# Latent attention on two sets of buffers, inverses on GpSimd's queue, and block 1's value, gate and key products in the wide form

## Chip, cores and metric

The kernel runs on one core of one Trainium2 chip. The metric is the time of one launch in microseconds of device time; a measurement is the median of several runs.

## What is computed

Two blocks one after the other on a sequence of 256 tokens with 2048 features, all in float32. The first has two layers, the second one. Cut to what the change touches:

```
u = rmsnorm(h) @ w_in[i]                       # block 1, each of 2 layers
a_val, a_glu, a_z, q, k, v, b_z = split(u)
a  = a_val * sigmoid(a_glu)
ya = silu(layernorm(conv31(a) + conv_b)) * silu(a_z)
yb = window_attention(q, k, v) * silu(b_z)
h  = h + concat(ya, yb) @ w_out[i];  h = h + e * sigmoid(h @ w_pg[i])
...
proj = rmsnorm(x) @ w_in_2                     # block 2
y_rwkv = rwkv7_mixer(...)                      # 16 heads of 64, a scan over tokens
y_mla  = mla_mixer(...)                        # 8 heads of 128, causal attention
x = x + concat(y_rwkv, y_mla) @ w_out_2
x = x + (silu(conv3(h @ w_gate)) * (h @ w_up)) @ w_down
```

## The kernel before

Features lie on the 128 partitions, the 256 tokens along the free dimension; 2048 features are 16 tiles ("k-tiles"). Every float32 product is made of two reduced-precision parts, high and low, of the weight and of the input: high x high, high x low and low x high.

**A product and its chunks.** A product of 256 outputs over 2048 inputs takes its weights in chunks of four k-tiles: SyncE fetches 512 KB into `wraw` (`chunks`, L289), ScalarE casts the high part `whi` (L285), VectorE subtracts it to get `wlo` (L286); there are four `wraw` buffers and three of each part. `lin` (L308) then issues, for each k-tile and each of two output tiles t, three matmuls of 256 columns into one bank: high x high, high x low, low x high (L327 to L329). `wide` (L332) issues for each k-tile and t one matmul of 512 columns, high weights against both parts of the input side by side (L347), and one of 256, low weights against the high part (L350), within a chunk first all high ones, then all low ones. Its result lies in two banks of PSUM, one per t, as two halves that have to be added. The first bank has the tag "lin", of which there are three; the second shares a tag with other work of its phase ("sc" in block 1, where the transposes of the input and the attention's scores use it as well). `fold` (L353) adds the halves: ScalarE copies one (L356), VectorE adds the other (L357), once per t. `add_wide` (L359) adds both to a tile on VectorE alone (L363).

**Block 1** (`layer1`, L502) makes per layer: eight products with `lin` for the values and gates of the convolution (`gated`, L486, multiplies them by the row scale, L494 and L495, and by the sigmoid), one with `lin` for the keys (L533), the value, query and gate products, the convolution's 31 taps on VectorE (L583, 480 instructions in all), the LayerNorm (mean L589 on TensorE, subtraction L593 on VectorE), then the products of the gates, the output and the embedding, all wide.

**Block 2's mixers** (`mixers`, L763) go through four groups G of heads. For each: projections (`rkv_lin`), `rwkv_prepare`, in which `tri_inverse` (L1036) inverts the groups' triangular 32 x 32 matrices, and `rwkv_chunks` (L1067), which walks over the tokens with many small products (pz, pch, po) and ends with the normalization (pgn, L1150) and the gate (pgt, L1163) and a write of the result to `ydr` in memory by GpSimd. `tri_inverse` writes the matrices to memory (xd), reads them back in another layout (eight reads to L), makes 31 steps on VectorE (L1058, L1059), writes the result (four writes to td, L1061) and reads it (Tc, L1063): 14 transfers, issued from ScalarE. Work of different groups and of the attention is put in order by a scheduler, which simulates a timeline, with a higher priority for the recurrence. Each engine and each queue does its work in the order that comes out.

The attention's eight heads are done in four pairs (`mla_pair`, L1249), all in one set of two buffers `mla_s`; a pair ends with the split of its output `yp` into high and low in `Ym`. Then the output projection adds to h, from `h2`, eight column groups of `Ym` (two chunks each), seven of the recurrence's first six k-tiles `Yr` (1.5 chunks each), and, when group 3's result has come back from `ydr` (`load_y(3)`), its two last k-tiles for these seven with `lin`, and the eighth group wide. The feed-forward follows: 44 wide products, and the last product with 512 columns a matmul. Eight large buffers ("x8") are shared by all of these in turn.

Of the kernel before, what the change touches and what calls it, by code (L numbers as in the profile page):

```python
# [18 lines left out]
SEQ = 256  # L19
# [97 lines left out]
class Kern:  # L117
# [214 lines left out]
    def wide(self, w, row0, kts, c0, S):  # L332
# [5 lines left out]
        for r, ks in self.chunks(w, row0, kts, c0, 2):  # L338
# [3 lines left out]
            for u in range(2):  # L342
                for t in range(2):
                    ts = slice(t * 128, t * 128 + 128)
                    for i, k in enumerate(ks):
                        if u == 0:
                            nc.tensor.matmul(ps[t][:], lhsT=hi[:, i, ts], rhs=S.both(k).rearrange("p u c -> p (u c)"),  # L347
                                             start=(k == kts[0]), stop=False)
                        else:
                            nc.tensor.matmul(ps[t][:, :SEQ], lhsT=lo[:, i, ts], rhs=S.hi(k), start=False, stop=(k == kts[-1]))  # L350
# [127 lines left out]
    def silu_pair(self, ps, r2, tag, bufs=2):  # L478

        nc = self.nc  # L480
        z = self.wk.tile([128, 2, SEQ], F32, tag=tag, bufs=bufs, name=self.nm("z"))
        nc.vector.tensor_tensor(z[:], ps[:], r2, ALU.mult)
        nc.scalar.activation(z[:], z[:], AF.Silu)
        return z

    def gated(self, pv, pg, r2, other):  # L486

        nc = self.nc
        sg = self.w1.tile([128, 2, SEQ], F32, tag="sg", name=self.nm("sg"))
# [4 lines left out]
        nc.vector.tensor_tensor(cur, pv[:], r2, ALU.mult)  # L494
        ins = nc.vector.tensor_tensor(sg[:], pg[:], r2, ALU.mult)  # L495
        if other is not None:
            self.behind(ins, other)
# [4 lines left out]
    def layer1(self, i, S, st):  # L502
# [12 lines left out]
        ps = []  # L515
        for j in range(8):
            ps.append(self.lin(w_in, 0, kall, (j % 2) * 1024 + j // 2 * 256, S))
            first = self.lo0
            if j % 2 == 0 and j > 0:
                apads.append(self.gated(*ps[j - 2 : j], r2, first))  # L520
                if (i, j) == (0, 2):
                    self.vectors(0)
                    self.bias_table()
                if i == 0:
                    self.bias_write(j // 2 - 1, self.gate)
        apads.append(self.gated(*ps[6:8], r2, None))
        if i == 0:
            self.bias_write(3, self.gate)
# [1049 lines left out]
```

## Time and profile before

| | us |
|---|---|
| median of 3 runs | 2218.68 (2218.06 to 2219.01) |
| profiled execution | 2222.46 |
| its span, first to last instruction | 2220.7 |
| TensorE busy | 2182.3 (98%) |
| weight loads busy | 1972.0 (89%) |
| VectorE busy | 1698.3 (76%) |
| ScalarE busy | 1186.7 (53%) |
| GpSimd busy | 106.7 (5%) |

The profiled execution is one of its own and took 3.78 us more than the median. Busy time of TensorE counts its matmuls with modelled ends, so neighbours overlap, and what a matmul costs in a dense run is the step from one start to the next. L347 in a row is line 347 of the code above. PE, DVE, ACT, POOL and SP are TensorE, VectorE, ScalarE, GpSimd and SyncE; "ACTq" and "POOLq" are their queues of DMA issues.

### The profile page before, as it was taken

The numbers are of one execution on the slowest core, as the hardware profiler recorded it, in microseconds if no ns is written. First come the engines' busy times: TensorE is split into PE (matmuls) and PEld (weight loads), VectorE is DVE, ScalarE is ACT, GpSimd is POOL, SyncE is SP. The second block draws the span as 40 slices with busy tenths as digits, with TensorE's granted clock in tenths as the row PEclk, the third lists the DMA queues.
The fourth block names the chain that finished last, engine by engine and source line by source line (L and its number), as shares of the span: only waits on it lengthen the run. The fifth ranks groups of instructions, "written<-read, shape, count | busy, mean of one in ns | idle before, by whom it ended". The sixth has DMA issues, their size and how long they took to land.

```text
span 2220.7 us, 37351 instructions
## 1 busy us (share of the span) xinstructions
PE 2182.3 (98%) x14263; PEld 1972.0 (89%) x14263; DVE 1698.3 (76%) x3140; ACT 1186.7 (53%) x1825; POOL 106.7 (5%) x253
## 2 busy tenths in 40 slices
PE   8999999999999999999999999999999999999998
PEld 8999988889999888899999887888888888888887
DVE  6999999778989988787777885777765576556765
ACT  6456746554456555656665655355443444444443
POOL 3100000000000000002100000010000000000000
PEclk9999999999999999999999998999999999999999
DMA  7875556665565466777665433576656666566654
GB/s 232 245 207 165 175 166 223 191 210 179 183 184 167 153 198 212 218 219 222 192 169 140 122 106 102 167 255 203 190 185 195 193 189 190 190 192 189 189 191 141
DMA packets 374514, 412.83 MB, mean 186 GB/s; under 512 B 40456, under 2 KB 327429, under 8 KB 373952
## 3 DMA queue, kind: packets, MB, share of 16 engines
q1 hardware_dynamic: 336464, 366.06, 53.6%
q0 software_dynamic: 10960, 31.79, 4.5%
q10 hardware_dynamic: 26912, 12.60, 2.6%
q8 instruction: 112, 1.84, 0.3%
q14 instruction: 66, 0.54, 0.1%
HBM read 390.47 MB, written 19.92 MB: 185 GB/s over the span
## 4 chain that ended last, share of the span: by engine, by line
PE 93%; DVE 3%; DMA 2%; ACT 1%; issue 1%; ACTq 0%; SPq 0%; DVEq 0%
PE wide L347 30%; PE wide L350 15%; PE lin L327 7%; PE lin L328 7%; PE lin L329 7%; PE lin L1393 3%; PE lin L1394 3%; PE lin L1392 3%; PE dn L1393 2%; PE dn L1394 2%; PE dn L1392 2%; PE po L701 1%; PE lin L1225 1%; PE lin L1223 1%; PE lin L1224 1%; DVE wlo L286 1%
## 5 line engine op out<-in xcount | busy, mean ns | idle before, releaser
L285 ACT CAST whi<-wraw 128x1024 fp32r<-128x1024 f32 (+1 forms) x708 | 724.8, 1026 | 837.7 <-PE wide L347 329.5
L286 DVE TENSOR_TENSOR wlo<-wraw,whi 128x1024 fp32r<-128x1024 f32 (+1 forms) x708 | 843.8, 1193 | 357.2 <-ACT whi L285 341.3
L347 PE MATMUL wide<-xs,whi 128*128 128x512 f32 x2916 | 745.7, 394 | 3.9 <-ACT whi L285 2.0
L347 PEld LDWEIGHTS wide<-xs,whi 128*128 128x128 f32 x2916 | 521.3, 189 | 95.0 <-ACT whi L285 2.5
L350 PEld LDWEIGHTS wide<-xs,wlo 128*128 128x128 f32 x2916 | 402.7, 190 | 33.0 <-DVE wlo L286 1.9
L350 PE MATMUL wide<-xs,wlo 128*128 128x256 f32 x2916 | 416.4, 283 | 0.4 <-DVE wlo L286 0.2
L329 PE MATMUL lin<-xs,wlo 128*128 128x256 f32 x1420 | 404.9, 285 | 2.2 <-DVE wlo L286 2.2
L327 PE MATMUL lin<-xs,whi 128*128 128x256 f32 x1420 | 405.5, 286 | 0.9 <-ACT whi L285 0.9
L328 PE MATMUL lin<-xs,whi 128*128 128x256 f32 x1420 | 404.7, 285 | 0.0
L329 PEld LDWEIGHTS lin<-xs,wlo 128*128 128x128 f32 x1420 | 273.5, 193 | 3.3 <-DVE wlo L286 2.6
L327 PEld LDWEIGHTS lin<-xs,whi 128*128 128x128 f32 x1420 | 273.4, 193 | 3.1 <-ACT whi L285 1.3
L328 PEld LDWEIGHTS lin<-xs,whi 128*128 128x128 f32 x1420 | 273.5, 193 | 1.1 <-issue 0.7
L583 DVE SCALAR_TENSOR_TENSOR cy<-apad,vc_cw,cy 128x256 f32<-128x256 f32 x480 | 229.7, 481 | 7.5
L1393 PE MATMUL lin<-wlo,xs 128*128 128x512 f32 (+1 forms) x304 | 117.7, 387 | 0.5 <-DVE wlo L286 0.5
L1394 PE MATMUL lin<-whi,xs 128*128 128x512 f32 (+1 forms) x304 | 117.0, 385 | 0.0
L1392 PE MATMUL lin<-whi,xs 128*128 128x512 f32 (+1 forms) x304 | 114.1, 386 | 0.2 <-ACT whi L285 0.2
L1393 PEld LDWEIGHTS lin<-wlo,xs 128*128 128x128 f32 x304 | 57.2, 188 | 11.9 <-DVE wlo L286 1.2
L1392 PEld LDWEIGHTS lin<-whi,xs 128*128 128x128 f32 x304 | 57.2, 188 | 11.6 <-ACT whi L285 0.6
L1392 PE MATMUL dn<-whi,xs 128*128 128x512 f32 (+1 forms) x176 | 67.0, 381 | 0.0
L1393 PE MATMUL dn<-wlo,xs 128*128 128x512 f32 (+1 forms) x176 | 67.0, 381 | 0.0
L1394 PE MATMUL dn<-whi,xs 128*128 128x512 f32 (+1 forms) x176 | 67.0, 381 | 0.0
L1394 PEld LDWEIGHTS lin<-whi,xs 128*128 128x128 f32 x304 | 57.2, 188 | 11.0
(540 smaller groups left out, 2374.4 us busy)
## 6 DMA issues: line engine op xcount, KB each, us to landing
wraw<-in_w_in_dram SPq DMA_DIRECT2D x244, 512.0 KB, 4.1
wraw<-in_w_out_dram SPq DMA_DIRECT2D x89, 512.0 KB, 4.2
wraw<-in_ffn_w_gate_dram SPq DMA_DIRECT2D x88, 512.0 KB, 4.4
wraw<-in_ffn_w_up_dram SPq DMA_DIRECT2D x88, 512.0 KB, 3.7
wraw<-in_ffn_w_down_dram SPq DMA_DIRECT2D x87, 512.0 KB, 3.9
wraw<-in_w_pg_dram SPq DMA_DIRECT2D x64, 512.0 KB, 4.3
bt<-btab POOLq DMA_DIRECT2D x32, 192.0 KB, 3.2
btab<-bF ACTq DMA_DIRECT2D x4, 1024.0 KB, 7.9
```

The source lines that it names most:

```text
L285: nc.scalar.copy(hi[:], src)
L286: self.lo = nc.vector.tensor_tensor(lo[:], src, hi[:].bitcast(F32), ALU.subtract)
L327: nc.tensor.matmul(ps[:, t, :], lhsT=h, rhs=xh_, start=((t, k) == first), stop=False)
L328: nc.tensor.matmul(ps[:, t, :], lhsT=h, rhs=xl_, start=False, stop=False)
L329: nc.tensor.matmul(ps[:, t, :], lhsT=l, rhs=xh_, start=False, stop=((t, k) == last))
L347: nc.tensor.matmul(ps[t][:], lhsT=hi[:, i, ts], rhs=S.both(k).rearrange("p u c -> p (u c)"), start=(k == kts[0]), stop=False)
L350: nc.tensor.matmul(ps[t][:, :SEQ], lhsT=lo[:, i, ts], rhs=S.hi(k), start=False, stop=(k == kts[-1]))
L583: prev, tail = tail, nc.vector.scalar_tensor_tensor(y, ap[:, t, k : k + SEQ], cw[:, k : k + 1], y, ALU.mult, ALU.add)
L701: nc.tensor.matmul(po[:, qb, g, :], lhsT=pT[:, kb, qb * 128 : qb * 128 + 128], rhs=vd[:, kb, j, :], start=(kb == 0), stop=(kb == 1))
L1392: nc.tensor.matmul(ps, lhsT=zh, rhs=hi, start=(k == 0), stop=False)
L1393: nc.tensor.matmul(ps, lhsT=zh, rhs=lo, start=False, stop=False)
L1394: nc.tensor.matmul(ps, lhsT=zl, rhs=hi, start=False, stop=(k == nt - 1))
```

## The change

Three parts. `wide` goes through a chunk of odd number with the low part first; start and stop of the accumulation are set by counting. Values, gates and keys of block 1 are wide products and are folded before the multiplication by the row scale. The attention has two sets of buffers, which pairs use in turn; a pair writes its output to `mdr` in memory over GpSimd's queue, and `Ym`, allocated after the pairs, is loaded from there as `Yr` is from `ydr`. The 14 transfers of an inverse are issued from GpSimd.

```diff
@@ wide
+        done = [0, 0]
+        for c, (r, ks) in enumerate(self.chunks(w, row0, kts, c0, 2)):
...
-            for u in range(2):
+            for u in ((0, 1) if c % 2 == 0 else (1, 0)):
...
+                        done[t] += 1
+                        flags = dict(start=(done[t] == 1), stop=(done[t] == 2 * len(kts)))
...
@@ value, gated (before: gated(pv, pg, r2, other))
+    def value(self, pv, r2):
...
+        cur = ap[:, :, 15 : 15 + SEQ]
+        self.fold(cur, pv)
+        nc.vector.tensor_tensor(cur, cur, r2, ALU.mult)
+        return ap
+    def gated(self, ap, pg, r2):
...
-        nc.vector.tensor_tensor(cur, pv[:], r2, ALU.mult)
-        ins = nc.vector.tensor_tensor(sg[:], pg[:], r2, ALU.mult)
+        self.fold(sg, pg)
+        nc.vector.tensor_tensor(sg[:], sg[:], r2, ALU.mult)
@@ layer1
+            ps = self.wide(w_in, 0, kall, (j % 2) * 1024 + j // 2 * 256, S)
...
+        self.fold(kT, self.wide(w_in, 0, kall, 4096, S))
+        nc.vector.tensor_tensor(kT[:], kT[:], r2, ALU.mult)
@@ mixers
-        self.mla_s = self.slot(F32, "mla"), self.slot(F32, "mla")
-        Ym = self.new_split(2)
+        self.mla_s = [(self.slot(F32, "mla"), self.slot(F32, "mla")) for _ in range(2)]
+        self.mdr = self.dr.tile([128, 8, SEQ], F32, name="mdr")
...
+        Ym = self.new_split(2)
+        h2 = [self.slot(F32, "h2") for _ in range(2)]
         Yr = self.new_split(2)
-        h2 = [self.slot(F32, "h2") for _ in range(2)]
...
+        for G in range(4):
+            load_y(G, Ym, self.mdr)
@@ tri_inverse (each of its 14 transfers)
-        nc.scalar.dma_start(xd[:].rearrange("(c q) j i -> (q j) c i", q=4), Lc[:])
+        nc.gpsimd.dma_start(xd[:].rearrange("(c q) j i -> (q j) c i", q=4), Lc[:])
@@ mla_pair
-        s1, s2 = self.mla_s
+        s1, s2 = self.mla_s[hp % 2]
...
-        self.split_pair(Y, 2 * hp, yp)
+        nc.gpsimd.dma_start(self.mdr[:, 2 * hp : 2 * hp + 2, :], yp)
```

**What it moves on TensorE.** The place is the end of the mixers, from the first product that needs group 3's inverse (pz on Ttr) on. Before: pz comes while the last pair's projections (`lin_2271`) and its attention are still ahead, and behind the last gate product (`pgt_2157`) wide products go on to the first `lin` of the last two k-tiles (`lin_2412`).

```order
L1307 MATMUL msc_2247_15379<-rope_10999,mla_2158_14849 128x256
L1082 MATMUL pz_2125_14659<-Ttr_2084_14416,XOc_2074_14311 32x32 x16
L1163 MATMUL pgt_2124_14652<-hg_10888,ga_2123_14649 128x256 x4
L1223 MATMUL lin_2271_15509<-whi_2265_15473,ck_1936_13276 128x256
...
L347 MATMUL wide_2343_15972<-xs_2161_14852,whi_2349_15998 128x512 x2
L1163 MATMUL pgt_2157_14842<-hg_10888,ga_2156_14839 128x256 x4
L347 MATMUL wide_2343_15972<-xs_2161_14852,whi_2349_15998 128x512 x2
...
L350 MATMUL wide_2400_16275<-xs_2281_15589,wlo_2406_16301 128x256 x2
L327 MATMUL lin_2412_16325<-xs_2281_15589,whi_2414_16328 128x256
```

Now: the last pair's attention (`mo_2293`, `mo_2297`) is done around that pz, and what follows are wide products alone (L353 and L355 are the high and the low part; in `wide_2311` the low part of the second chunk comes first).

```order
L1330 MATMUL mo_2293_15068<-mla_2179_14366,mla_2178_14365 128x128
L1331 MATMUL mo_2293_15068<-mla_2179_14366,mla_2178_14365 128x128
L1332 MATMUL mo_2293_15068<-mla_2179_14366,mla_2178_14365 128x128
L1085 MATMUL pz_2143_14173<-Ttr_2102_13930,XOc_2092_13825 32x32 x16
L1330 MATMUL mo_2297_15093<-mla_2179_14366,mla_2178_14365 128x128
L1331 MATMUL mo_2297_15093<-mla_2179_14366,mla_2178_14365 128x128
L1332 MATMUL mo_2297_15093<-mla_2179_14366,mla_2178_14365 128x128
L353 MATMUL wide_2312_15152<-xs_2298_15099,whi_2315_15157 128x512 x4
L355 MATMUL wide_2312_15152<-xs_2298_15099,wlo_2316_15158 128x256 x4
```

Now, the end: the normalization and the gate product of group 3 (`pgt_2175`) stand behind the last wide product, `wide_2424`, and the next row is `lin_2436`, on the two last k-tiles.

```order
L353 MATMUL wide_2423_15803<-xs_2303_15104,whi_2429_15829 128x512 x2
L353 MATMUL wide_2424_15804<-xs_2303_15104,whi_2429_15829 128x512
L1153 MATMUL pgn_2173_14345<-cblk_72,Y_2145_14215 128x128 x4
L353 MATMUL wide_2424_15804<-xs_2303_15104,whi_2429_15829 128x512
L1166 MATMUL pgt_2175_14356<-hg_10402,ga_2174_14353 128x256 x4
L327 MATMUL lin_2436_15854<-xs_2303_15104,whi_2438_15857 128x256
L327 MATMUL lin_2440_15880<-xs_2303_15104,whi_2442_15883 128x256
L327 MATMUL lin_2445_15908<-xs_2303_15104,whi_2447_15911 128x256
```

What moved: attention ahead of chunk 3, and the wide products that stood behind the last gate product ahead of it.

**What it moves on GpSimd's queue.** The place is the same, from the write of group 1's result on. Before, GpSimd issues the results' writes and reads, the gate's weights and h, and nothing of the inverse.

```order
L1166 DMA ydr_10760<-sq_1927_13236 128x512
L833 DMA sq_2285_15614<-ydr_10760 128x512
L1158 DMA ga_2156_14839<-in_rwkv_g2_2_dram 128x256
L1159 DMA ga_2156_14839<-in_rwkv_g2_2_dram 64x256
L1166 DMA ydr_10760<-sq_2117_14620 128x512
L827 DMA h2_2282_15590<-hdr_260 128x2048
L827 DMA h2_2283_15591<-hdr_260 128x2048
L833 DMA sq_2286_15618<-ydr_10760 128x512
L1166 DMA ydr_10760<-sq_2150_14810 128x512
L833 DMA sq_2407_16316<-ydr_10760 128x512
```

Now, around group 3's inverse (td, Tc), which shares the queue with the attention's outputs (mdr) and h2:

```order
L828 DMA h2_2300_15101<-hdr_260 128x2048
L1334 DMA mdr_14367<-mla_2177_14364 128x512
L828 DMA h2_2301_15102<-hdr_260 128x2048
L834 DMA sq_2304_15123<-mdr_14367 128x512
L1334 DMA mdr_14367<-mla_2179_14366 128x512
L834 DMA sq_2305_15127<-mdr_14367 128x512
L1064 DMA td_2096_13847<-T_2099_13860 256x1x32 x4
L1334 DMA mdr_14367<-mla_2177_14364 128x512
L1161 DMA ga_2174_14353<-in_rwkv_g2_2_dram 128x256
L1162 DMA ga_2174_14353<-in_rwkv_g2_2_dram 64x256
L1169 DMA ydr_10274<-sq_2135_14134 128x512
L1066 DMA Tc_2101_13929<-td_2096_13847 128x8x32
```

What moved: the four writes of td stand behind the reads of the first two pairs' outputs, and Tc behind the third pair's and a result's write.

## Rows read from the trace of the kernel before

**Rows 1.** The page of the profiled execution: busy time and share of each engine; the clock that was granted to TensorE in 40 equal slices (tenths of full speed); the chain of work that ended last, by engine and by line.
```profile
PE 2182.3 (98%) x14263; PEld 1972.0 (89%) x14263; DVE 1698.3 (76%) x3140; ACT 1186.7 (53%) x1825; POOL 106.7 (5%) x253
PEclk9999999999999999999999998999999999999999
...
PE 93%; DVE 3%; DMA 2%; ACT 1%; issue 1%; ACTq 0%; SPq 0%; DVEq 0%
PE wide L347 30%; PE wide L350 15%; PE lin L327 7%; PE lin L328 7%; PE lin L329 7%; PE lin L1393 3%; PE lin L1394 3%; PE lin L1392 3%; PE dn L1393 2%; PE dn L1394 2%; PE dn L1392 2%; PE po L701 1%; PE lin L1225 1%; PE lin L1223 1%; PE lin L1224 1%; DVE wlo L286 1%
```

**Rows 2.** Timeline of TensorE in block 1, a product of `lin`: start, duration (pipelined, so longer than the step), line, operation.
```profile
200.05 0.28 PE L328 MATMUL lin<-xs,whi 128*128 128x256 f32 x1
200.17 0.28 PE L329 MATMUL lin<-xs,wlo 128*128 128x256 f32 x1
```

**Rows 3.** Timeline of TensorE in block 1, a product of `wide`; each row is one run of matmuls (x8 is 2 output tiles by 4 input tiles).
```profile
447.83 1.11 PE L350 MATMUL wide<-xs,wlo 128*128 128x256 f32 x8
448.78 2.00 PE L347 MATMUL wide<-xs,whi 128*128 128x512 f32 x8
450.62 1.12 PE L350 MATMUL wide<-xs,wlo 128*128 128x256 f32 x8
453.42 0.28 PE L350 MATMUL wide<-xs,wlo 128*128 128x256 f32 x1
```

**Rows 4.** Timeline of TensorE in the feed-forward's last product, 512 columns each.
```profile
1943.90 0.39 PE L1393 MATMUL dn<-wlo,xs 128*128 128x512 f32 x1
1944.13 0.39 PE L1394 MATMUL dn<-whi,xs 128*128 128x512 f32 x1
```

**Rows 5.** Windows by stage: length, busy time of each engine with its instructions, mean granted clock of TensorE, share of the DMA engines, GB/s. 1120 to 1418 us are the mixers from group 2's inverse on and the attention, 1418 to 1470 the output projection.
```profile
1120.00:1240.00 120.00, 116.22 (x1041) 109.05 (x1039) 92.10 (x284) 71.12 (x128) 7.02 (x17) 0.99 0.51 136
1240.00:1337.00 97.00, 90.70 (x760) 81.77 (x759) 77.36 (x262) 59.75 (x135) 4.78 (x9) 0.93 0.41 113
1337.00:1418.00 81.00, 76.79 (x485) 64.77 (x486) 52.48 (x117) 38.22 (x80) 3.22 (x6) 0.89 0.40 127
1418.00:1470.00 52.00, 51.18 (x312) 44.68 (x310) 41.80 (x78) 24.86 (x39) 4.90 (x9) 1.00 0.63 205
```

**Rows 6.** The same view for block 1's first layer up to the LayerNorm.
```profile
40.00:330.00 290.00, 289.62 (x2066) 272.47 (x2064) 263.93 (x490) 160.25 (x247) 21.45 (x48) 1.00 0.65 192
```

**Rows 7.** The page's costliest groups of instructions: the 512-column matmul of `wide` over the whole span.
```profile
L347 PE MATMUL wide<-xs,whi 128*128 128x512 f32 x2916 | 745.7, 394 | 3.9 <-ACT whi L285 2.0
```

**Rows 8.** Instructions by line, ScalarE: the copy of `fold` in the gates of block 1 (count, busy us, mean ns of one).
```profile
L356 ACT COPY z<-wide 128x256 f32<-128x256 f32 x16 | 5.1, 374 | 0.0
```

**Rows 9.** The same for VectorE: the add of `fold`, and the multiply that reads a product of `lin`.
```profile
L357 DVE TENSOR_TENSOR z<-z,wide 128x256 f32<-128x256 f32 x16 | 6.2, 413 | 0.0
L494 DVE TENSOR_TENSOR apad<-lin,r 128x512 f32<-128x512 f32 x8 | 5.5, 690 | 2.2 <-PE lin L329 1.3 <-ACT r L251 1.0
```

**Rows 10.** The chain, 320 to 345 us: start, duration, work. VectorE's subtraction of the LayerNorm's mean, behind the sums of the convolution.
```profile
327.75 2.48 DVE cy L593 x4
```

**Rows 11.** Window of the first 20 us, TensorE.
```profile
0.00:20.00 20.00, 13.41 (x75) 1.00 0.94 294
```

**Rows 12.** Timeline of TensorE at the start: two matmuls of `lin` at the slower step of the first 14 us.
```profile
13.29 0.41 PE L327 MATMUL lin<-xs,whi 128*128 128x256 f32 x1
13.51 0.41 PE L328 MATMUL lin<-xs,whi 128*128 128x256 f32 x1
```

**Rows 13.** The output tile of group 3 behind its last gate product pgt: by instruction count, durations (min/median/max, ns) and start times (first and last) between 1418 and 1432 us.
```profile
L1165 DVE TENSOR_TENSOR sq<-sq,pgt x1: 690/690/690, 1420.5 to 1420.5; 128x512 f32<-128x512 f32 x1
L1166 POOL DMA_DIRECT2D ydr<-sq x1: 553/553/553, 1421.7 to 1421.7; - x1
L272 DVE TENSOR_TENSOR xs<-sq,xs x1: 692/692/692, 1429.6 to 1429.6; 128x512 fp32r<-128x512 f32 x1
```

**Rows 14.** Timeline of TensorE: the first `lin` on the output of group 3.
```profile
1452.18 0.28 PE L327 MATMUL lin<-xs,whi 128*128 128x256 f32 x1
```

**Rows 15.** Timeline of GpSimd: the issue of a transfer with 256 runs.
```profile
17.46 0.74 POOL L718 DMA_DIRECT2D pr<-in_p_dram  x1
```

**Rows 16.** The inverse's matrix T in memory: its four writes and its read per group, as issued by ScalarE's queue (durations as above).
```profile
L1061 ACTq DMA_DIRECT2D td<-T x16: 571/628/638, 1130.5 to 1326.9; - x16
L1063 ACTq DMA_DIRECT2D Tc<-td x4: 378/385/392, 1137.0 to 1332.1; - x4
```

**Rows 17.** Windows of ten microseconds, TensorE alone: busy time, granted clock.
```profile
1260.00:1270.00 10.00, 8.26 (x71) 0.85 0.67 161
1370.00:1380.00 10.00, 9.81 (x54) 0.69 0.17 49
```

**Rows 18.** The chain, group 3's inverse: the last write of T, its read, and the second of the products (pz) behind it.
```profile
1326.89 5.17 DMA td<-T
1332.08 2.37 DMA Tc<-td
...
1344.56 1.46 PE pz L1094 x30
```

**Rows 19.** Transfers by kind: queue, count, size, median us from issue to landing.
```profile
ydr<-sq POOLq DMA_DIRECT2D x4, 256.0 KB, 3.2
...
L<-xd ACTq DMA_DIRECT2D x16, 32.0 KB, 3.9
...
Tc<-td ACTq DMA_DIRECT2D x4, 128.0 KB, 2.4
```

More of the change, by code (lines that the diff above doesn't have):

```diff
@@ L341, in wide @@
                 hi, lo = self.wsplit(r[:, :n, :], [128, n, 256])
[L342 removed]
+            if ks[0] == kts[0]:
+                self.lo0 = self.lo
+            for u in ((0, 1) if c % 2 == 0 else (1, 0)):
                 for t in range(2):
@@ L345, in wide @@
                     for i, k in enumerate(ks):
+                        done[t] += 1
+                        flags = dict(start=(done[t] == 1), stop=(done[t] == 2 * len(kts)))
                         if u == 0:
-                            nc.tensor.matmul(ps[t][:], lhsT=hi[:, i, ts], rhs=S.both(k).rearrange("p u c -> p (u c)"),
-                                             start=(k == kts[0]), stop=False)
+                            nc.tensor.matmul(ps[t][:], lhsT=hi[:, i, ts], rhs=S.both(k).rearrange("p u c -> p (u c)"), **flags)
                         else:
-                            nc.tensor.matmul(ps[t][:, :SEQ], lhsT=lo[:, i, ts], rhs=S.hi(k), start=False, stop=(k == kts[-1]))
+                            nc.tensor.matmul(ps[t][:, :SEQ], lhsT=lo[:, i, ts], rhs=S.hi(k), **flags)
         return ps
@@ L493, in gated @@
         cur = ap[:, :, 15 : 15 + SEQ]
-        nc.vector.tensor_tensor(cur, pv[:], r2, ALU.mult)
-        ins = nc.vector.tensor_tensor(sg[:], pg[:], r2, ALU.mult)
-        if other is not None:
-            self.behind(ins, other)
+        self.fold(cur, pv)
+        nc.vector.tensor_tensor(cur, cur, r2, ALU.mult)
+        return ap
+    def gated(self, ap, pg, r2):
+        nc = self.nc
+        sg = self.w1.tile([128, 2, SEQ], F32, tag="sg", name=self.nm("sg"))
+        cur = ap[:, :, 15 : 15 + SEQ]
+        self.fold(sg, pg)
+        nc.vector.tensor_tensor(sg[:], sg[:], r2, ALU.mult)
         self.gate = nc.scalar.activation(sg[:], sg[:], AF.Sigmoid)
@@ L514, in layer1 @@
         apads = []
-        ps = []
         for j in range(8):
[L517 to L528, printed above, removed]
+            ps = self.wide(w_in, 0, kall, (j % 2) * 1024 + j // 2 * 256, S)
+            if j % 2 == 0:
+                apads.append(self.value(ps, r2))
+                continue
+            self.gated(apads[-1], ps, r2)
+            if (i, j) == (0, 1):
+                self.vectors(0)
+                self.bias_table()
+            if i == 0:
+                self.bias_write(j // 2, self.gate)
         V = self.v1[i]
-        pk = self.lin(w_in, 0, kall, 4096, S)
         kT = self.w1.tile([128, 2, SEQ], F32, tag="sg", name=self.nm("kT"))
-        nc.vector.tensor_tensor(kT[:], pk[:], r2, ALU.mult)
+        self.fold(kT, self.wide(w_in, 0, kall, 4096, S))
+        nc.vector.tensor_tensor(kT[:], kT[:], r2, ALU.mult)
         half = lambda ap, h: ap[64 * h : 64 * h + 64]
@@ L830, in mixers, with load_y @@
                                                ALU.mult, ALU.mult)
-        def load_y(G):
+        def load_y(G, dst, src):
             yt = self.sqt()
-            nc.gpsimd.dma_start(yt[:], self.ydr[:, 2 * G : 2 * G + 2, :])
-            self.split_pair(Yr, 2 * G, yt[:])
+            nc.gpsimd.dma_start(yt[:], src[:, 2 * G : 2 * G + 2, :])
+            self.split_pair(dst, 2 * G, yt[:])
+        for G in range(4):
+            load_y(G, Ym, self.mdr)
         for G in range(3):
-            load_y(G)
+            load_y(G, Yr, self.ydr)
         def rows(k0, k1, j, Y, row0=0):
@@ L849, in mixers @@
             rows(0, 6, j, Yr)
-        load_y(3)
+        load_y(3, Yr, self.ydr)
         vf = self.vf
```

21 lines of the change are left out of this document (6 added, 15 removed).

## The prediction

> **What bounds the kernel now.** I read the page's busy shares, its 40 slices and the chain first. TensorE is busy for 98% of the span, at nearly full clock, and the chain that ends last is 93% TensorE, two thirds of it the products of `wide` and `lin` [rows 1]. So time can come from three places only: TensorE work that costs less, stretches where TensorE is idle or clocked down, and new stalls of either kind. Then I read the timeline for the step from one matmul to the next, since a busy engine's true price is its cadence: in `lin` a 256-column matmul follows every 0.120 us [rows 2]; in `wide` a chunk of eight 512-column and eight 256-column matmuls comes every 1.84 + 0.95 us, 2.795 from run to run [rows 3]; a dense run of 512-column matmuls has 0.227 us [rows 4]. Last the windows by stage, for idle time and clock: 1120 to 1418 us, mixers and latent attention, is the one long stretch that loses some [rows 5].
>
> **Products made wide.** Eight value and gate products and one key product per layer become wide: 18 products of 4 chunks, 72 chunks. A chunk of `lin` is 24 matmuls, 24 x 0.120 = 2.88 us; a wide one is 2.795, or 2.785 in the alternating order (next part). The difference, 0.085 to 0.095 us, times 72 is 6.1 to 6.8, with the 0.7 that a whole switch fewer would add at most 7.5; I take **-7.0 us**. This is on the path, since nothing but TensorE's own work sets the pace there (289.6 of 290 us busy from 40 to 330 us [rows 6]).
>
> By a rule of the Trainium skill ("TensorE: Matmul & The Clock Gate", section "Back-to-back issue gap") an isolated matmul of N columns takes N/2.4 + 2.5 ns, so a wide pair would save only one 2.5 ns overhead: an estimate of 576 x 2.5 ns = 1.4 us in place of 7. The rows give 0.120 and 0.227, some 13 ns over N/2.4 in each, so the rows decide.
>
> **The alternating order.** Chunk 2 now begins with the low part, on which chunk 1 ended, so a product switches widths half as often. Two switches a chunk cost what a chunk takes beyond its parts: 2.795 - (8 x 0.227 + 8 x 0.120 = 2.776) = 0.019 us. Half of it, 0.0095, over some 365 chunks (2916 recorded 512-column matmuls, 8 a chunk [rows 7]) is 3.5; some runs are cut by other work anyway, so **-3.0 us**. Bounds: 0 (the 0.019 may come from the chunk's own change of weights) and -7 (all of it). That odd chunks ask for the low weights first costs nothing while VectorE's split runs a chunk ahead; if it falls behind, the wait comes before the high half in place of after it, at most 1.84 us earlier each time.
>
> **The fold.** A wide result is in two banks and has to be added up: two ScalarE copies of 0.372 [rows 8] and two VectorE adds of 0.413 [rows 9], against one VectorE multiply of 0.690 that read the bank and stays as a multiply from SBUF. Issued back to back two adds take about 0.74, so 18 products add 13.3 us to VectorE and about 12 to ScalarE, half per layer. ScalarE has the room. VectorE is busy 263.9 of 290 us before the first LayerNorm [rows 6], so 6.7 us fit into 26, but not all of the 26 is free at the right place: the convolution's last sums end just ahead of the LayerNorm, where TensorE already waits behind four 0.68 us operations [rows 10]. Bounds: 0 and all 6.7 us plus the wait, 9 a layer. I take 1 per layer, near the lower end because the row shows slack there, **+2**.
>
> **Start.** Before, 256-column matmuls of `lin` fill TensorE between the input's transposes; it is busy 13.4 of the first 20 us [rows 11]. A wide product's second bank has the tag "sc", which the transposes use too, so it starts after the last transpose: ahead of that one the order had 49 matmuls of `lin` as filler and has 16 of `wide` now. 49 x 0.17 (between the step of 0.12 and the 0.22 of the first 14 us [rows 12]) = 8.3 us against 8 x 0.227 + 8 x 0.12 = 2.8 gives the upper bound, 5.5; the lower is 0, if the input's arrival sets the end anyway. I take the middle, **+2.5**, as no row tells which.
>
> **The mixers.** Three edits act together: two sets of attention buffers, attention's output through memory instead of straight into Ym, and the inverses' 14 transfers each on GpSimd's queue. What can be won: idle time plus (1 - clock) x length in the three windows [rows 5], that is 3.8 + 1.2, 6.3 + 6.8 and 4.2 + 8.9, **31.2 us** in all. The orders of the change show that pairs 1 and 2 are projected earlier and that all attention is over ahead of group 3's second pz, with chunk 3 then woven into dense wide products. A dense stretch of that kind is 1418 to 1470: 51.2 of 52 us busy, clock 1.00 [rows 5]. So of the last 13.1 about 10 go; of the 13.1 before, I take half; of the first 5, half: -10 - 6.5 - 2.5 = -19.
>
> What comes new: before, some 32 us of wide products (1420.5 to 1452.2 us) follow the last gate product pgt, and under them its result is multiplied, written, read back and split. That takes from 1420.5 to 1430.3, 9.8 us [rows 13], and nobody waits for it: the first `lin` on it runs at 1452.18 [rows 14]. In the new order `lin` on just this data follows pgt at once, and no wide product is left. So that latency is exposed, **+9.5** (it was 9.8, of which the last part needs only the second half of the split; bounds 8 and 12, the upper with a clock that falls in the hole).
>
> GpSimd's queue: a transfer's issue takes GpSimd 0.55 us with 128 runs [rows 13] and 0.74 with 256 [rows 15], so about 0.2 us per 128 short runs; ScalarE took 0.57 to 0.64 for 256 and 0.38 for Tc [rows 16]. An inverse has 1024 runs in xd and in Tc, 512 in each of four and 256 in four more: about 13 us of GpSimd, some 7 more than on ScalarE. Bounds: 0, where group 3 is not what the end waits for, and +7. ScalarE in turn is rid of 56 issues of 0.38 to 0.64, some 28 us; that buys between 0 and 5. I let these two cancel. What the moved instructions now stand behind, in one queue: two 1024 KB h2 loads, the mdr writes and their reads, each of which waits for attention. What used to wait behind them on ScalarE's, casts of weights, waits no longer. Mixers together: -19 + 9.5 = **-9.5**.
>
> **The sum.** -7.0 - 3.0 + 2 + 2.5 - 9.5 = -15.0. The profiled execution took 2222.46 us (span 2220.7), so about 2207.5 by its own measure; it stands 3.8 above the median of the three runs, 2218.68. I forecast **2204 us** for the median.
>
> **Rivals.**
> 1. *More is won in the mixers.* If the pairs fill nearly all holes, 28 of the 31.2 us go, and the exposed latency is partly covered by the other columns' wide chunks: 2218.7 - 5.5 - 28 + 7 = about 2192. For it: the clock there is down to 0.69 to 0.85 in ten-microsecond windows [rows 17], and the dense stretch behind them ran at 1.00. Against it: holes ahead of 1240 us come from the chain of the inverses, not from attention.
> 2. *Counts only.* The mixers give nothing net: holes are moved to other places, or the 9.5 us and the 7 of the queue eat the rest; 2218.7 - 5.5 = 2213. For it: most of the 31.2 us lie where several short chains share TensorE, and the trace doesn't show that more buffers would shorten any of them. Against it: the largest loss, 13.1 us after 1337, is beside attention that will be over by then.
> 3. *Slower: group 3's inverse gets stuck in GpSimd's queue.* The order puts two mdr reads and one mdr write, which wait for pairs 0 and 1, ahead of the four td writes, and Tc behind another mdr write and a ydr write. Before, the way from the last td write to the second pz took from 1326.9 to 1344.6 us [rows 18], and the end had 32 us in reserve. Now the end has none: each microsecond by which td or Tc is late shows whole. If pair 1's and 2's outputs are late by a scores-softmax-values round and the reads land 3.2 us later each, Tc is 25 us late, and the time is 2204 + 25 = about 2229. From 15 us of lateness the gain is gone, from 19 it is slower. Against it: pairs 1 and 2 are projected early in the new order.
>    The Trainium skill ("SBUF — State Buffer", section "SBUF: two separate sides") names a mechanism that would do the same: descriptors of GpSimd's transfers are written by GpSimd, which is shut out while VectorE runs certain copies, and it advises ScalarE's queue instead. The trace so far does not bear it out: with VectorE 76% busy GpSimd's transfers land in 3.2 us, ScalarE's in 2.4 to 3.9 [rows 19].
> 4. *VectorE becomes the bound before LayerNorm.* 9 us a layer in place of 1: 2204 + 16 = 2220.
>
> **How the numbers follow.** A measurement of this kernel tells 0.2%, 4.4 us, from no change, so "same" is 2214.2 to 2223.1. Chances: the forecast with its bounds (2198 to 2211) 0.54, rival 1 0.18, rival 2 0.15, rival 3 0.07, rival 4 0.06. Faster: 0.54 + 0.18 + 0.11 of rival 2 = 0.83; same: 0.04 + 0.06 = 0.10; slower 0.07. The range leaves out rival 3 and the far half of rival 1 and of rival 4: 2185 to 2217.
>
> **What would show it.** Right: `lin`'s rows in block 1 gone, the wide cadence 2.78 us in pairs of chunks; TensorE idle some 9 us between pgt and the next `lin`, the one large hole; clock 1.00 through chunk 3's last 70 us. Wrong: TensorE waiting for Ttr (Tc) or for VectorE ahead of cs; a long wait of GpSimd ahead of td; a first wide product that ends past where `lin` did by more than 5 us.

## The result and the profile after

The change takes **2241.2 us** (median of 4 runs, 2239.0 to 2242.7) where the kernel before took 2218.4 beside it: a ratio of 1.0102, with a 95% interval of 1.0089 to 1.0114. The forecast was 2204 (2185 to 2217), so the sign was wrong (forecast -15, measured +22.8). The profiled execution took 2242.3, its span 2240.5.

The page after, to be read against [rows 1]: TensorE does less (2179.9 us in place of 2182.3, 576 matmuls fewer in the records), and yet the span is longer.

```profile
PE 2179.9 (97%) x13687; PEld 1944.6 (87%) x13687; DVE 1715.5 (77%) x3176; ACT 1207.8 (54%) x1861; POOL 146.4 (7%) x317
```

**What went as forecast.** The wide cadence in block 1 (timeline of TensorE, against [rows 3]): two chunks from 453.83 to 459.39, 2.78 us each.

```profile
453.83 3.82 PE L353 MATMUL wide<-xs,whi 128*128 128x512 f32 x16
457.48 2.08 PE L355 MATMUL wide<-xs,wlo 128*128 128x256 f32 x16
459.39 1.78 PE L353 MATMUL wide<-xs,whi 128*128 128x512 f32 x7
```

The latency behind the last gate product, which 32 us of wide products used to cover [rows 14], is exposed: 8.26 us of idle TensorE, then some 23 `lin` matmuls at 0.21 in place of 0.12 us, 2.2 us more, until 1474.05 (in brackets: the idle time of the engine before a row, and what ended it).

```profile
1458.26 2.58 PE L1166 MATMUL pgt<-hg,ga 128*128 128x256 f32 x8 [0.88 <-ACT sq L1158]
1469.10 1.01 PE L327 MATMUL lin<-xs,whi 128*128 128x256 f32 x3 [8.26 <-ACT xs L271]
1474.05 0.34 PE L327 MATMUL lin<-xs,whi 128*128 128x256 f32 x1
```

**What did not.** TensorE in windows of 40 us (length, busy time with its matmuls, granted clock, DMA share, GB/s), first before, then after. In the windows from 1320 and 1440 TensorE is now idle for 9.5 and 9.1 us, where it was for 2.7 and 3.0, and what came free ahead of 1240 is small.

```profile
1120.00:1160.00 40.00, 38.07 (x333) 0.96 0.65 165
1320.00:1360.00 40.00, 37.29 (x287) 0.87 0.55 165
1440.00:1480.00 40.00, 37.04 (x230) 1.00 0.70 231
```

```profile
1120.00:1160.00 40.00, 40.00 (x375) 1.00 0.69 193
1320.00:1360.00 40.00, 30.52 (x210) 0.91 0.51 168
1440.00:1480.00 40.00, 30.87 (x181) 0.87 0.45 143
```

A ledger of the span, worked out from such windows of 20 us: idle TensorE plus (1 - clock) x length, by part of the program. Where a low clock falls on idle time it counts twice, so the last row, the span less all such loss (what little lies outside these parts too), is only near the work's own price.

```
us                      before   alt  wide  ACT queue  after
start, 0 to 40             6.6   6.6   7.7        7.6    7.5
LayerNorm 1, 320 to 380    2.7   2.9   8.7        8.7    8.7
LayerNorm 2, 800 to 860    1.1   1.3   8.4        8.4    7.6
mixers, 1120 to 1520      34.6  17.1  18.7       37.0   46.9
end, from 2140            11.7  13.7  14.2       14.0   15.1
rest of the span        2163.6 2163.0 2156.7  2155.8  2153.8
```

(alt, wide and ACT queue are e_alt, e_wide and e_after_actq below.) From before to after the rest falls by 9.8, about the 10 us of the two count terms; 12.5 come at the LayerNorms, 3.4 at the end, and 12.3 in the mixers, where 9.5 were to be won. How far the last row can be trusted: 0.6 of the 9.8 falls with the alternating order, 6.3 with the wide products, and 2.9 between e_wide and the change, which have the same products; in the kernels below that have the products of e_wide it lies between 2151.9 and 2159.1.

### The profile page after: what moved, and what is told of

The parts are those of the page before. It is cut to its first block, busy times and chain, and to the rows that moved or that the text cites. A ratio compares the mean times of both kernels' runs of the same rounds, so it can differ in the third digit from the quotient of the medians.

```text
span 2240.5 us, 36345 instructions
## 1 busy us (share of the span) xinstructions
PE 2179.9 (97%) x13687; PEld 1944.6 (87%) x13687; DVE 1715.5 (77%) x3176; ACT 1207.8 (54%) x1861; POOL 146.4 (7%) x317
## 5 line engine op out<-in xcount | busy, mean ns | idle before, releaser
L353 PE MATMUL wide<-xs,whi 128*128 128x512 f32 x3492 | 857.6, 394 | 14.3 <-DVE xs L272 8.1
L353 PEld LDWEIGHTS wide<-xs,whi 128*128 128x128 f32 x3492 | 638.5, 189 | 139.1 <-DVE xs L272 8.6
L355 PEld LDWEIGHTS wide<-xs,wlo 128*128 128x128 f32 x3492 | 454.8, 191 | 27.0 <-DVE wlo L286 5.5
L355 PE MATMUL wide<-xs,wlo 128*128 128x256 f32 x3492 | 466.3, 284 | 4.2 <-DVE wlo L286 3.2
L327 PE MATMUL lin<-xs,whi 128*128 128x256 f32 x844 | 241.6, 287 | 8.9 <-ACT xs L271 8.3
L329 PE MATMUL lin<-xs,wlo 128*128 128x256 f32 x844 | 241.8, 287 | 0.0
L328 PE MATMUL lin<-xs,whi 128*128 128x256 f32 x844 | 241.0, 286 | 0.0
L327 PEld LDWEIGHTS lin<-xs,whi 128*128 128x128 f32 x844 | 162.5, 193 | 10.3 <-ACT xs L271 8.7
L329 PEld LDWEIGHTS lin<-xs,wlo 128*128 128x128 f32 x844 | 162.5, 193 | 1.6 <-issue 1.3
L328 PEld LDWEIGHTS lin<-xs,whi 128*128 128x128 f32 x844 | 162.5, 193 | 0.9 <-issue 0.3
```

What stands on the lines that cost most here:

```text
L327: nc.tensor.matmul(ps[:, t, :], lhsT=h, rhs=xh_, start=((t, k) == first), stop=False)
L328: nc.tensor.matmul(ps[:, t, :], lhsT=h, rhs=xl_, start=False, stop=False)
L329: nc.tensor.matmul(ps[:, t, :], lhsT=l, rhs=xh_, start=False, stop=((t, k) == last))
```

## The experiments

The kernel before was run beside each and took 2218.5 to 2220.0; ratios are to it.

**1. The change in layers.** e_alt is the kernel before with the alternating order alone; e_wide adds the wide values, gates and keys and leaves the mixers; e_after_actq is the whole change but for the inverse's queue; e_after_oneset the whole but for attention's sets and its way through memory.

```diff
@@ e_alt, to before
-            for u in range(2):
+            for u in ((0, 1) if c % 2 == 0 else (1, 0)):
...
@@ e_wide, to e_alt
+        self.fold(cur, pv)
+        self.fold(sg, pg)
+            ps = self.wide(w_in, 0, kall, (j % 2) * 1024 + j // 2 * 256, S)
+        self.fold(kT, self.wide(w_in, 0, kall, 4096, S))
...
@@ e_after_actq, to the change (L1047 to L1066)
-            nc.gpsimd.dma_start(td[:, :, q, :], T[32 * q : 32 * q + 32, :, :])
+            nc.scalar.dma_start(td[:, :, q, :], T[32 * q : 32 * q + 32, :, :])
...
@@ e_after_oneset, to the change
-        nc.gpsimd.dma_start(self.mdr[:, 2 * hp : 2 * hp + 2, :], yp)
+        self.split_pair(Y, 2 * hp, yp)
...
```

> The kernel before with the alternating order alone. Theory counts (the order saves half of the width switches, 0.0125 us a chunk as the trace of the change shows, some 365 chunks): 4 to 4.5 us faster, about 2214, and nothing else moved: VectorE's LayerNorm stalls as before. Rival (the mixers' order is sensitive to any change of the products' times): 125 wide matmuls stand behind the last pgt in place of 182, still enough to hide 10 us, so a loss there would speak for the rival.

Measured: 2208.4, 0.9947 [0.9932, 0.9963].

> Alternating order and the wide value, gate and key products, mixers as before. Theory fold (block 1's two LayerNorm stalls, 5 and 6 us longer in the trace of the change, come with the folds on VectorE and ScalarE): -4.5 - 7 + 1.7 (start) + 11.5 = +2, about 2220 with TensorE idle or clocked down some 9 to 10 us around each LayerNorm. Rival (the stalls are only an accident of the full change's order): 2209, stalls of 3 us as before.

Measured: 2215.9, 0.9979 [0.9967, 0.9990].

> The full change with the inverse's 14 transfers back on ScalarE's queue: wide products and two sets of buffers stay. In its order 186 wide matmuls stand behind the last pgt again, in place of 0. Theory queue (moving the transfers made group 3 late and left nothing behind pgt): the 17 us later first lin goes, 2241 - 20 = about 2220 or less, no 8 us hole ahead of the first lin. Rival sets (two sets put the attention ahead of group 3's inverse and make it late whatever the queue): still 2232 or more.

Measured: 2235.3, 1.0067 [1.0052, 1.0083].

> The full change with one set of attention buffers and Ym split directly, as before; wide products and GpSimd's queue stay. In its order 99 wide matmuls stand behind the last pgt, 17 us, enough for the 9.8 us. Theory queue: the inverses are late by the same 13 to 20 us on VectorE, part of it is covered, about 2230. Rival sets: about 2220, group 3's pz back at 1340 to 1350 us.

Measured: 2222.4, 1.0009 [0.9993, 1.0024].

So the steps are -11.7 for the order of chunk parts, +7.5 for the wide products, +19.4 for sets and memory, +5.9 for the queue on top of them (7.8 by the ratios, since the change itself was timed beside another set of runs of the kernel before). e_alt gained nearly three times what was expected. At the LayerNorms e_wide loses 8.7 and 8.4 us in the ledger, as the theory on the fold had it. Of the other two, both came out as the rival on the sets said. Most of the loss is the sets' and memory's, and the fastest kernel of all is e_alt.

**2. Sets or memory?** e_oneset_mem is e_wide with attention's output through memory and one set; e_sets_yrfirst is e_after_actq with the products of Yr, the recurrence's result, ahead of those of Ym, attention's. In both the allocation moves along: Ym's buffers are taken only behind the pairs, in the second behind Yr and h2.

```diff
@@ e_oneset_mem, to e_wide
-        self.split_pair(Y, 2 * hp, yp)
+        nc.gpsimd.dma_start(self.mdr[:, 2 * hp : 2 * hp + 2, :], yp)
...
@@ e_sets_yrfirst, to e_after_actq (its loads load_y are moved likewise)
-        for j in range(8):
-            rows(0, 8, j, Ym, 1024)
...
+        for j in range(8):
+            rows(0, 8, j, Ym, 1024)
```

> Wide products, inverses on ScalarE's queue, one set of attention buffers as before, but the pair's output goes through memory and Ym is allocated after the pairs, as in the change: of the part on latent attention only the second set is taken away. Theory filler (two sets let all four pairs' projections run early, by 1331 us, so that nothing is left to cover the softmaxes and the last inverse): back to the time of the kernel with wide products alone, 2216, within 5 us. Rival round trip (write, read and split of a pair's output, 8 to 10 us each, keep the first products of the output projection waiting): 2228 to 2236, stalls of TensorE between 1320 and 1400 us of 20 us or more.

Measured: 2233.9, 1.0061 [1.0039, 1.0083].

> Wide products, two sets, inverses on ScalarE's queue; the output projection begins with the recurrence's six k-tiles (Yr, in the memory of ck and a recurrence buffer), and the attention's part (Ym) comes second. The first 29 us of wide products then need no attention. Theory filler: TensorE's stalls between 1320 and 1400 us, 33 us with two sets, fall to under 20, and the time from 2235 to 2222 or less. Rival: if the hole is the in-order wait of VectorE for the attention's softmaxes (T's steps stand behind them), it stays at 2230 or more. Only 79 wide matmuls stand behind the last pgt, 13 us, just enough for its 9.8.

Measured: 2227.9, 1.0039 [1.0024, 1.0054].

The way through memory costs nearly what both did (18 us over e_wide, with one set); the second set on top of it adds 1.4, less than these runs can tell. So my theory that two sets let attention run ahead and leave TensorE without filler isn't needed for the 18 us. It isn't refuted either: e_sets_yrfirst came out between what it said (2222 or less) and what its rival said (2230 or more), and two sets without the way through memory weren't tried. What memory does, in e_oneset_mem's list of waits (engine, waiter, releaser: us, times, longest); in e_wide's the first row has 4.5 us, and the second is absent:

```profile
DVE xs L272 <- ACT xs L271: 11.5, 9, 3.2
ACT xs L271 <- DMA sq<-mdr: 10.2, 3, 4.8
```

ScalarE stands at the cast (L271) until the read of `mdr` lands, and VectorE at the subtraction (L272) until the cast is done; what the program has put behind these two, casts and splits of weights among it, stands with them (TensorE's waits for whi and wlo between 1120 and 1520: 8.7 us, in e_wide 4.7).

**3. How much of it is that standing?** Both are e_oneset_mem with Yr first; e_mem_once also reads all of `mdr` in one transfer after the last pair, so that no split stands in line early.

```diff
@@ e_mem_four, to e_oneset_mem: the edit of e_sets_yrfirst
@@ e_mem_once, to e_mem_four
+        nc.gpsimd.dma_start(ya[:], self.mdr[:])
-            load_y(G, Ym, self.mdr)
+            self.split_pair(Ym, 2 * G, ya[:, 2 * G : 2 * G + 2, :])
...
```

> One set of buffers, attention's output through memory in four reads as in the change, wide products, ScalarE's queue; the output projection begins with Yr's products. Companion of the next kernel. With Ym first the same parts took 2234. Theory waits in line (the four splits stand in ScalarE's and VectorE's queues between softmaxes and casts, and each waits 2 to 5 us there for its read): 2226 to 2234, since the splits still stand there. Rival late products (it is the first wide products that wait for Ym): Yr first gives them 29 us of cover, so 2218 or less.

Measured: 2224.6, 1.0024 [1.0012, 1.0037].

> As its companion, but attention's output is read back in one transfer behind the last pair, so that none of the four splits can stand in the queues ahead of the last pair's softmaxes. Theory waits in line: ScalarE's waits on the read between 1320 and 1380 us go, TensorE's stalls from 1320 to 1400 us (22 with Ym first) fall to 10 to 14 and the time to 2216 to 2222, below its companion by 5 or more. Rival late products: no better than the companion, or worse by the longer read.

Measured: 2219.1, 0.9989 [0.9976, 1.0002].

e_mem_four came out between its two expectations, so both have a part; e_mem_once did what the theory said. Of the 18 us, then, some 9 (7.4 in e_sets_yrfirst) go with Ym's products being first in line, 5.5 with splits that wait in the queues, and 3 stay. Each of these edits also changes the scheduler's order, and experiment 5 will show that this alone can move as much; what speaks for the reading is that the wait goes along with the time: ScalarE stands for `mdr` for 10.2 us in e_oneset_mem, for 6.3 in e_mem_four, and not at all in e_mem_once's list. TensorE's window from 1360 tells the same, e_mem_four above e_mem_once:

```profile
1360.00:1400.00 40.00, 36.89 (x235) 0.87 0.37 114
```

```profile
1360.00:1400.00 40.00, 39.29 (x273) 1.00 0.48 158
```

With two sets it isn't that clean. The mixers' loss in the ledger, 1120 to 1520, split into its two parts:

```
us      before  e_alt  e_wide  oneset_mem  mem_four  mem_once  sets_yrfirst  ACT queue  after
idle      17.2   12.1    13.5        21.6      16.9      12.3          14.4       20.0   29.7
clock     17.4    5.0     5.2        15.6      13.8       7.0          17.2       17.0   17.2
```

In the kernels with the way through memory and a loss over e_wide, the change itself excepted, more than half of that loss is a lower granted clock. And e_sets_yrfirst, whose list has no wait of ScalarE for `mdr` and whose TensorE is idle hardly longer than e_wide's, still takes 12 us more than e_wide. By the ledger nearly all of that is clock: from 1330 to 1380 it is at 0.61 to 0.83, between its two levels (1.00 and 0.50, 2.4 and 1.2 GHz), and in the first 20 us of that TensorE was idle for 6.6:

```profile
1330.00:1340.00 10.00, 7.76 (x38) 0.83 0.32 103
1340.00:1350.00 10.00, 5.67 (x20) 0.68 0.17 38
```

Whether the second set or only the order that comes with it makes that hole isn't shown.

**4. The fold.** e_wide_pool has the values' and gates' multiply by the row scale on GpSimd; e_wide_pool_lin also the first product in `lin` again.

```diff
@@ e_wide_pool, to e_wide
-        nc.vector.tensor_tensor(cur, cur, r2, ALU.mult)
+        nc.gpsimd.tensor_tensor(cur, cur, r2, ALU.mult)
-        nc.vector.tensor_tensor(sg[:], sg[:], r2, ALU.mult)
+        nc.gpsimd.tensor_tensor(sg[:], sg[:], r2, ALU.mult)
@@ e_wide_pool_lin, to e_wide_pool
+            if (i, j) == (0, 0):
+                apads.append(self.value(self.lin(w_in, 0, kall, 0, S), r2))
+                continue
...
```

> Alternating order and wide value, gate and key products, mixers as before, with the multiplications of values and gates by the row scale on GpSimd (16 of 128x512). They take 11 us off VectorE, most of what the folds put on it. Theory fold (VectorE's extra work delays the last convolution sums and with them both LayerNorms): TensorE's stalls around 320 to 360 and 800 to 840 us, 9.4 and 8.4 with the folds, go back to 4.5 and 2.3; about 2206 against 2216. Rival (the order of the products and of their ScalarE copies): stalls stay, 2215.

Measured: 2212.8, 0.9973 [0.9958, 0.9988].

> As the kernel with the row scale on GpSimd, with the very first product (values, layer 0) as lin again, whose matmuls fill TensorE between the transposes of the input. Theory start (the wide form's second bank shares its tag with the transposes): stalls in the first 40 us 7 in place of 10.4, 3 us faster than its companion. Rival: the input's arrival sets the end of this stretch, no difference.

Measured: 2212.7, 0.9967 [0.9953, 0.9980].

With VectorE relieved, the loss at the second layer's LayerNorm falls from 8.4 us in the ledger to 3.4 in both kernels. At the first layer's it is cut by half in e_wide_pool (8.7 to 4.6), but back at 9.8 in e_wide_pool_lin, where the clock fell; there more than the fold decides. The windows, e_wide, e_wide_pool and e_wide_pool_lin:

```profile
320.00:360.00 40.00, 34.66 (x197) 30.25 (x196) 34.74 (x70) 23.51 (x41) 3.45 (x8) 0.91 0.52 170
```

```profile
320.00:360.00 40.00, 35.87 (x216) 31.32 (x215) 35.55 (x70) 27.12 (x46) 3.45 (x8) 1.00 0.60 188
```

```profile
320.00:360.00 40.00, 35.39 (x196) 31.23 (x195) 33.67 (x66) 26.13 (x45) 3.42 (x8) 0.87 0.53 171
```

Of the whole time little is left: 3.2 us by the medians, 1.3 by the ratios, whose intervals overlap, where the theory had 10; in the mixers e_wide_pool loses 24.6 us to e_wide's 18.7. The start's `lin` gains nothing that can be measured (0.1 us).

**5. Why is e_alt so good?** By the steps the cadence pays some 4 us; 11.7 came. The feed-forward shows the cadence alone: between the first `dn` of its first and last groups lie 112 wide chunks, which take 476.05 us in the kernel before (1656.68 to 2132.73) and in e_alt_b, 474.93 in e_alt (1643.23 to 2118.16) and e_alt_ac: 0.010 us a chunk, 3.7 for 365. The alternating order in block 1 and the feed-forward alone (e_alt_ac), and in the mixers' stage alone (e_alt_b):

```diff
@@ e_alt_ac and e_alt_b, to e_alt
-            for u in ((0, 1) if c % 2 == 0 else (1, 0)):
+            for u in ((0, 1) if c % 2 == 0 or self.ph == "b" else (1, 0)):
+            for u in ((0, 1) if c % 2 == 0 or self.ph != "b" else (1, 0)):
```

> Alternating order in block 1 and in the feed-forward only; the wide products of the mixers' stage keep high before low. The alternating kernel was 11.7 us faster, of which the steps explain 4.5. Theory order (the products' shorter times let the planner put group 3's chunk differently, 125 wide matmuls behind the last pgt in place of 182; the stalls there fell by 8): this kernel has that order too, so about 2209, stalls from 1320 to 1400 us 9 in place of 21. Rival form (in the mixers' stage itself the alternation lets odd chunks wait less): about 2214 to 2216.

Measured: 2209.9, 0.9954 [0.9939, 0.9969].

> Alternating order in the mixers' stage only (the output projection's wide products, some 30 chunks, 0.4 us by the steps). Its order around group 3 is that of the kernel before (183 wide matmuls behind the last pgt). Theory order: 2218, no difference. Rival form: about 2210, stalls from 1320 to 1400 us 9.

Measured: 2219.0, 0.9999 [0.9989, 1.0010].

e_alt_ac doesn't touch the code of the mixers' stage, and yet their loss in the ledger falls from 34.6 to 17.3 (e_alt_b: 33.9). The scheduler puts another order together: 125 wide matmuls stand behind the last pgt in place of 182; the others run ahead of it. Both came out as the theory on the order said.

**6. The queue by itself.** e_wide with the inverse's way in (xd, L) or out (td, Tc) on GpSimd's queue.

```diff
@@ e_q_in, to e_wide
-        nc.scalar.dma_start(xd[:].rearrange("(c q) j i -> (q j) c i", q=4), Lc[:])
+        nc.gpsimd.dma_start(xd[:].rearrange("(c q) j i -> (q j) c i", q=4), Lc[:])
...
@@ e_q_out, to e_wide
-            nc.scalar.dma_start(td[:, :, q, :], T[32 * q : 32 * q + 32, :, :])
+            nc.gpsimd.dma_start(td[:, :, q, :], T[32 * q : 32 * q + 32, :, :])
...
```

> Wide products and one set of buffers with a direct split (2216 with the inverse on ScalarE's queue, 2222 with all 14 transfers on GpSimd's); here the nine transfers into the inverse (xd, L) are GpSimd's, the five out of it (td, Tc) ScalarE's. In its order VectorE's first T step stands 21 to 25 rows behind Lc for groups 1 to 3, 10 to 12 with all on ScalarE's queue. Theory order (the planner expects these transfers later than they come, and VectorE does other rows first): most of the 6 us, 2219 to 2223; the first T step of group 2 some 5 us or more later behind Lc than the 14.3 with ScalarE's queue, and without a wait, since L has landed. Rival transfers out (the reads and writes of T are what is late): 2216 to 2217.

Measured: 2236.7, 1.0080 [1.0065, 1.0095].

> The reverse: xd and L on ScalarE's queue, td and Tc on GpSimd's. First T steps 9 to 11 rows behind Lc, as with all on ScalarE's queue. Theory order: 2214 to 2218. Rival transfers out: 2220 or more, with the way from td to Ttr longer by 2 us or more a group.

Measured: 2223.9, 1.0028 [1.0016, 1.0039]; its runs lie between 2217.8 and 2227.6, and the profiled one is the first of these, so that its trace doesn't show the median.

The way in costs 20.7, the way out 8, and both together 6.5 (e_after_oneset against e_wide). A price per transfer would add up; these don't. Neither theory fits both kernels: e_q_in is slower than either said, e_q_out is where the rival had it. In the traces 9 to 13 of VectorE's rows lie between a group's Lc and its first step T with ScalarE's queue (groups 1 to 3), 27 to 37 with all on GpSimd's, 22 to 26 in e_q_in, 9 to 12 in e_q_out: the scheduler places the chain anew each time. In e_q_in's trace TensorE stands for group 3's Ttr, for 6.94 us (in e_wide 0.9 for all four groups): T's four writes, on ScalarE's queue as in e_wide, land 3.4 to 9.4 us after they are issued (e_wide: 2.4 to 3.7), and Tc is read only then:

```profile
1358.81 1.73 PE L1082 MATMUL pz<-Ttr,XOc 32*32 32x32 f32 x32 [6.94 <-DVE Ttr L1064]
1358.31 0.45 DVE L1064 STREAM_TRANSPOSE Ttr<-Tc 128x256 f32<-128x256 f32 x1 [7.71 <-DMA Tc<-td]
```

Why they land that late isn't shown.

## Why the prediction was wrong

**Right.** The counts: 2.78 us a chunk measured, 0.010 us a chunk for the alternating order (forecast 0.0095), and the rest of the span 9.8 shorter (forecast 10). That last match is in part luck, as the ledger tells this row to 3 or 4 us only. From e_alt to e_wide the rest falls by 6.3 (forecast 7.0). By the estimate from the Trainium skill's "TensorE: Matmul & The Clock Gate" ("Back-to-back issue gap") the wide products would save 1.4 us; the rows were the better guide. The start: +0.9 in the ledger (forecast +2.5, bounds 0 and 5.5). The exposed latency: 8.3 idle + 2.2 of clock (forecast 9.5, bounds 8 to 12).

**Mis-sized: the fold.** Forecast +1 a layer; the ledger has +6.0 and +6.5, inside the bound of 9; they come with the wide products (e_alt to e_wide: +5.8 and +7.1). In the trace after, ahead of the first LayerNorm, VectorE has hardly a gap and is late with wlo and with cy; TensorE waits:

```profile
326.42 0.74 PE L355 MATMUL wide<-xs,wlo 128*128 128x256 f32 x4 [1.02 <-DVE wlo L286]
330.23 0.70 PE L589 MATMUL cs<-cy,cblk 128*128 128x256 f32 x2 [0.72 <-DVE cy L583]
333.58 0.38 PE L1226 MATMUL lin<-pp,whi 128*128 128x256 f32 x1 [2.66 <-ACT ev L741]
```

The 26 us of slack were a mean over 290 us; at that place there was none, which the four operations of [rows 10] had already said. (The 0.372 us of a fold's copy is 0.374 in [rows 8]; nothing hangs on it.) The queue, whose two terms were left to cancel, cost 5.9 to 7.8 us on top of the rest.

**The step that failed** is "So of the last 13.1 about 10 go; of the 13.1 before, I take half", the -19 of the mixers. In the ledger the loss there didn't shrink to some 25 (34.6 - 19 + 9.5) but grew to 46.9; without the exposed latency, some 36 in place of 15.6. It was argued from what the two sets free. What wasn't priced is the way through memory, put at nothing in the sum: its split is an instruction in ScalarE's queue and one in VectorE's, placed by a simulated timeline, and when the read lands later than that, all behind it waits. The chip's timeline of VectorE after, group 3's T steps (L1061, L1062) among the scaling of h (L830) and the splits (L272):

```profile
1336.48 0.22 DVE L1061 TENSOR_TENSOR Tt<-L,T 128x66 f32<-128x66 f32 x1
...
1338.34 3.25 DVE L830 SCALAR_TENSOR_TENSOR h<-h,vc_a,rf 128x256 f32<-128x256 f32 x8
...
1341.97 0.22 DVE L1062 TENSOR_TENSOR T<-T,Tt 128x66 f32<-128x66 f32 x1
...
1342.70 0.68 DVE L272 TENSOR_TENSOR xs<-sq,xs 128x512 fp32r<-128x512 f32 x1
...
1345.07 0.21 DVE L1061 TENSOR_TENSOR Tt<-L,T 128x48 f32<-128x48 f32 x1
1348.42 0.69 DVE L272 TENSOR_TENSOR xs<-sq,xs 128x512 fp32r<-128x512 f32 x1 [3.15 <-ACT xs L271]
1349.03 0.20 DVE L1062 TENSOR_TENSOR T<-T,Tt 128x48 f32<-128x48 f32 x1
```

Between the two halves of one T step lie 5.5 us, for the scaling of h among others, and later 4.0, for a split that can't start. ScalarE's row says what that one waits for, and TensorE's rows what both cost: its next wide chunks in line are Ym's. The first of them waits for a split that stands behind that scaling, the second for the read.

```profile
1347.77 0.62 ACT L271 CAST xs<-sq 128x512 fp32r<-128x512 f32 x1 [3.07 <-DMA sq<-mdr]
```

```profile
1343.44 2.08 PE L353 MATMUL wide<-xs,whi 128*128 128x512 f32 x4 [5.71 <-DVE xs L272]
1349.16 0.73 PE L353 MATMUL wide<-xs,whi 128*128 128x512 f32 x2 [1.94 <-DVE xs L272]
```

These 7.65 us are most of what the window from 1320 lacks. Experiments 2 and 3 show the cause for one set of buffers: 18 us with the way through memory, 3 left when Ym goes last and nothing waits in line. For the change itself, with two sets, it is shown in part: the rows above and 7.4 us from Ym going last; what makes the 12 us that e_sets_yrfirst keeps over e_wide, mostly clock, stays open. Two of the signs that the prediction named for being wrong came: the wait of TensorE for VectorE ahead of cs (0.72 us above) and GpSimd's long wait ahead of td (below).

**Rival 3 had the sign and half of the size (2229), but not its mechanism.** T does come late: td is issued at 1354.2 to 1355.8 in place of 1324.9 to 1326.9 [rows 16], Ttr comes at 1364.1, and the second pz starts at 1372.9 in place of 1344.6 [rows 18], 28 us later (rival 3 said 25). But GpSimd's queue doesn't hold it; GpSimd issued the read of `mdr` at 1344.49 and then stood idle for 9.14 us until VectorE's last T step.

```profile
1344.49 0.54 POOL L834 DMA_DIRECT2D sq<-mdr  x1 [4.70 <-DMA mdr<-mla]
1354.16 2.30 POOL L1064 DMA_DIRECT2D td<-T  x4 [9.14 <-DVE T L1062]
1360.81 0.92 POOL L1066 DMA_DIRECT2D Tc<-td  x1
```

What I held against it, that pairs 1 and 2 are projected early, says nothing on who else stands in VectorE's queue. The rule of the Trainium skill that I set beside it ("SBUF — State Buffer", "SBUF: two separate sides") isn't borne out after the change either: with VectorE 77% busy GpSimd's transfers of T land in 1.9 us, of Tc in 3.9; on ScalarE's queue before, they took 3.7 and 2.4.

```profile
td<-T POOLq DMA_DIRECT2D x16, 32.0 KB, 1.9
Tc<-td POOLq DMA_DIRECT2D x4, 128.0 KB, 3.9
```

Rival 2 was right in its words, that no row showed more buffers to shorten any chain; rival 4 came two thirds true (12.5 of its 18 us).

## What to carry to other kernels

A transfer put between a producer and its consumer also puts the consumer's first instructions into in-order queues: ask what stands behind them and how late the data can be, and give them a place at which the data has long landed. Idle time in a stretch of short chains isn't won by a resource unless a row shows a wait for that resource. And where a scheduler sets the order, test each edit alone: here the edit with the least to it gave all the gain (e_alt, 0.9947), and what was added to it lost 33 us.

## What the runs showed that was not expected

- The order that comes out of the scheduler moves the time by as much as the edits do: e_alt_ac won 8.7 us, by the ledger in a stage whose code it leaves alone (17.3 us less loss there), and the inverse's queue cost 20.7, 8 or 6.5 us depending on which transfers went along.
- GpSimd issues Tc's 1024 short runs in 0.92 us (row above); from [rows 13] and [rows 15] I had worked out 0.2 per 128, some 1.9. The 14 issues of an inverse take it some 9.5 us by their medians, where I had 13.
- In e_after_actq TensorE's granted clock was 0.59 and 0.60 in two windows of 20 us, nearer the lower of its two levels (0.50, 1.2 GHz) than the upper (1.00, 2.4 GHz), behind ten microseconds of which TensorE was idle for 4.9; in the next window it was 1.00:

```profile
1330.00:1340.00 10.00, 5.09 (x35) 0.93 0.67 219
1340.00:1360.00 20.00, 16.48 (x50) 0.59 0.17 41
1360.00:1380.00 20.00, 18.84 (x142) 0.60 0.14 49
1380.00:1400.00 20.00, 18.08 (x133) 1.00 0.36 119
```
